# Moving a transformer layer's SBUF tiles so that every TensorE operand starts at a multiple of 256 bytes

## The chip, the core and the metric

The kernel runs on one core of one Trainium2 chip. The metric is device time in microseconds (us) of one execution; three runs of the kernel before gave 862.43, 862.78 and 863.02 us, and their median, 862.78 us, is the time before. A nanosecond (ns) is a thousandth of a us. The five engines are called PE (TensorE), DVE (VectorE), ACT (ScalarE), POOL (GpSimd) and SP (the engine that issues most DMAs). SBUF is the on-chip memory: 128 partitions, and in each a tile takes a run of bytes that begins at the same byte in all of them. That first byte is what this change is about.

## The reference, cut to what matters

```python
u = rms_norm(x, mix_norm_g)                       # x: 512 tokens x 1024 features, float32
q, k, v, cf_val, cf_gate, sc_x, sc_b, sc_c, gates = split(u @ w_in)
y_a = stick_breaking_attention(norm(q), norm(k), v) @ w_attn_out     # 8 heads of 64
hb  = silu(layer_norm(causal_conv_31(cf_val * sigmoid(cf_gate)) + dw_b))
y_b = hb @ w_conf_out
y_c = (sc_b * causal_conv_3(sc_c * sc_x)) @ w_sc_out
g   = sigmoid(gates + gate_b)
x   = x + (g[0] * y_a + g[1] * y_b + g[2] * y_c) @ w_o
gt, up = split(rms_norm(x, ffn_norm_g) @ w_ffn_in)                   # inner width 2816
x   = x + (silu(gt) * up) @ w_ffn_out
```

## The kernel before, in words

Every product is made of float32r operands: a float32 operand is split into a high and a low part (`split_to`, L75), and `mm3` (L87) multiplies high by high, high by low and low by high into one PSUM bank. In the profile the operands stand in the order moving, stationary: in `mm<-u,wh` the tile `u` streams through the array, 512 columns of it, while 128 columns of `wh` sit in it as weights. Each matmul comes with its own weight load (PEld in the profile).

Two helpers make nearly all matmuls. `unit` (L140) multiplies one block of 128 weight columns: the weights `wh` and `wl` are stationary, the activations move, in 24 matmuls where the contraction has 8 blocks of 128 and 12 where it has 4. `rows_product` (L629) and `values` (L364) do it the other way: activations are stationary and the weights move. The tiles on the activation side are

- `u` (16 tiles): the normed input, later the feed-forward's input. 96 units of 24 matmuls move it, and `values` holds it stationary in 96 matmuls: 2400 in all.
- `m` and `b` (18 and 8 tiles): everything else, that is queries and keys, the branches' inputs `oT`, `hb` and `hc`, the merged sum and the feed-forward's inner activations. 288 matmuls (three branches, 8 units of 12) move them, and `rows_product` holds them stationary in 720 (192 for `w_o`, 528 for `w_ffn_out`): 1008 in all.
- attention's own `l0`, `l1`, `l2`, `a` and `v`, and the constants `identr`, `big_ident`, `neg_tri`, `neg_ones`, `head_mean`; these take part in short matmuls of 128, 256 and 384 columns and in some 70 of 512.

PE's order is the order of the calls (`manual_schedule`, L163): input projections and the first norms, attention mixed with other units (`tick`, L99), the three branches, the output projection `w_o`, then twice a half of the feed-forward's input units and its `w_ffn_out`. The other engines are ordered by a scheduler with priorities. Weights come by DMA into `raw` (three buffers), ACT casts them to `wh`, DVE subtracts to `wl`.

Tiles are placed in the order in which their pools are opened, and within a pool in the order in which their tags first occur; each takes a whole number of 32 bytes. The kernel's first free byte is 16,512. Pool `cst` (L48) comes first and holds constants and parameter columns of odd sizes (4, 232, 496, 32, 16 bytes); pool `sb` (L49) follows with everything else. In `sb`, the tags `c` and `cf` have tiles of 2056 bytes (512 + 2 floats) and 2168 bytes (512 + 30 floats); all others are multiples of 512 bytes. So `cst` sets where `sb` begins, and each group of `c` or `cf` tiles shifts what follows it.

Of the kernel before, what the change touches and what calls it, by code (L numbers as in the profile page):

```python
# [8 lines left out]
F32 = mybir.dt.float32  # L9
F32R = mybir.dt.float32r  # L10
# [4 lines left out]
P = 128  # L15
S = 512
D = 1024
KT = D // P
# [3 lines left out]
EPS = 1e-6  # L22
# [13 lines left out]
def hybrid_layer(ctx, tc, x, mix_norm_g, w_in, q_norm_g, k_norm_g, w_attn_out, conf_dw_w,  # L36
                 conf_dw_b, conf_ln_g, conf_ln_b, w_conf_out, sc_conv_w, w_sc_out, gate_b,
                 w_o, ffn_norm_g, w_ffn_in, w_ffn_out, out):
    """Every product runs on the tensor engine as float32r operands: a float32 operand is the
    exact sum of a high and a low part of 12 significant bits each, and three passes  # L40
    (high*high, high*low, low*high) carry the product at float32's accuracy."""
    nc = tc.nc
    x, w_in, w_o = x[0], w_in[0], w_o[0]
    w_attn_out, w_conf_out, w_sc_out = w_attn_out[0], w_conf_out[0], w_sc_out[0]
    w_ffn_in, w_ffn_out, out = w_ffn_in[0], w_ffn_out[0], out[0]

    pool = lambda name, **kw: ctx.enter_context(tc.tile_pool(name=name, **kw))
    cst = pool("cst", bufs=1)  # L48
    sb = pool("sb", bufs=1)  # L49
    ps = pool("ps", bufs=1, space=PSUM)  # L50
    BUFS = {"raw": 3, "wh": 3, "wl": 3, "u": 16, "m": 18, "b": 8, "v": 2, "cf": 5, "c": 4, "t": 6,
            "s": 2, "a": 4, "l0": 2, "l1": 1, "l2": 1, "mm": 4, "z": 3, "o": 1}
# [1 line left out]

    def alloc(tag, shape=(P, S), dt=F32):
        count[0] += 1
        where = ps if tag in ("mm", "z", "o") else sb
        return where.tile(list(shape), dt, tag=tag, name=f"{tag}_{count[0]}", bufs=BUFS[tag])

    def psum(tag="mm"):  # L60
        return alloc(tag)

    def tmp(dt=F32, shape=(P, S)):
        return alloc("t", shape, dt)
# [4 lines left out]
    def exp_log():  # L69
        table(nc.scalar.preload_act_table_set("natural_log_exp_and_others"))  # L70

    def act(o, i, f, **kw):
        table(nc.scalar.activation(o, i, f, **kw))  # L73
# [10 lines left out]
    def mm(o, lhsT, rhs, start, stop):  # L84
        nc.tensor.matmul(o, lhsT, rhs, start=start, stop=stop, skip_group_check=True)  # L85

    def mm3(o, a, b, start, stop):  # L87
        mm(o, a[0], b[0], start, False)
        mm(o, a[0], b[1], False, False)
        mm(o, a[1], b[0], False, stop)  # L90

    # ---- the tensor engine's order is the order of the calls below: units of products come
    # from a queue in steps of one contraction block, with other products in between ----
    queue, later = [], []

    def defer(steps, fn):
# [23 lines left out]
        return  # L120
        yield

# [1 line left out]
    def raw(src, kt, width):  # L124
        with tc.high_priority():
            t = alloc("raw", (P, kt, width))
            nc.sync.dma_start(t, src.rearrange("(k p) n -> p k n", p=P))
        return t
# [3 lines left out]
    def wsplit(src):  # L132
        nsplit[0] += 1
        kt, n = src.shape[1], src.shape[2]
        with tc.high_priority():
            hi, lo = alloc("wh", (P, kt, n), F32R), alloc("wl", (P, kt, n), F32R)
            split_to(hi, lo, src, sub=nc.gpsimd.tensor_sub if nsplit[0] in POOLW else None)
        return hi, lo

    def unit(src, j, a, done):  # L140
        src, a = src(), a()
        w = wsplit(src[:, :, j * P:(j + 1) * P])
        kt = src.shape[1]
        o = psum()
        for k in range(kt):
            mm3(o, (w[0][:, k, :], w[1][:, k, :]), a[k], k == 0, k == kt - 1)
            if k == kt - 1:
                done(o)
            yield
# [12 lines left out]

    ctx.enter_context(tc.manual_schedule(engines={mybir.EngineType.PE}))  # L163

# [1 line left out]
    def load_x(tag):  # L166
        t = []
        for i in range(NT):
            t.append([alloc(tag) for _ in range(2)])
            for n in range(2):  # L170
                nc.sync.dma_start(t[i][n], x[i * P:(i + 1) * P, n * S:(n + 1) * S])  # L171
        return t
# [6 lines left out]

    rows_w = alloc("s", (P, P))  # L180
    rows = alloc("s", (P, P))
    rows_g = cst.tile([KT, P], F32, name="rows_g")
    nc.scalar.dma_start(rows_g, mix_norm_g[0].rearrange("(k p) -> k p", p=P))
    at = {}
    r = 0
# [16 lines left out]

    ident_f = alloc("c", (P, P))
    make_identity(nc, ident_f)
    identr = cst.tile([P, P], F32R, name="identr")
    nc.gpsimd.tensor_copy(identr, ident_f)
    ident = identr.bitcast(F32)
    big_ident = cst.tile([P, P], F32R, name="big_ident")
    nc.gpsimd.tensor_scalar_mul(big_ident, ident_f, BIG)
    eps = cst.tile([P, 1], F32, name="eps")  # L210
    nc.gpsimd.memset(eps, EPS)
# [10 lines left out]
        return cols[:, at[name] + i:at[name] + i + 1]  # L222

    def const(name, fill):
        t = cst.tile([P, P], F32R, name=name)
        f = tmp(shape=(P, P))
        fill(f)
        nc.gpsimd.tensor_copy(t, f)
        return t
# [13 lines left out]
            nc.gpsimd.memset(f[h * 64:(h + 1) * 64, h * 64:(h + 1) * 64], 1.0 / 64)  # L243

    def rsqrt(y, m, w):
        """y = (m + EPS) ** -0.5, one Newton step after the table's value; w: two tiles like y."""
        t, s = w
        act(t, m, AF.Ln, bias=eps)
        act(y, t, AF.Exp, scale=-0.5)
        nc.scalar.activation(s, y, AF.Square)  # L250
        nc.vector.scalar_tensor_tensor(t, m, eps, s, ALU.add, ALU.mult)
        nc.vector.tensor_scalar(t, t, -0.5, 1.5, ALU.mult, ALU.add)
        nc.vector.tensor_mul(y, y, t)

# [1 line left out]
    exp_log()  # L256
    transpose_rows(cols_g, rows_g, KT)
    uT = [(alloc("u", dt=F32R), alloc("u", dt=F32R)) for _ in range(KT)]
# [22 lines left out]
    neg_ones = const("neg_ones", filled(-1.0))  # L281
    head_mean = const("head_mean", heads)

# [1 line left out]
    cf = []  # L285
    marks = []

# [12 lines left out]
    gates = [unit(cfg[i // 2], i % 2, U, cf_gate) for i in range(CT)]  # L300
# [7 lines left out]
    transpose_rows(cols_w, rows_w, nw)  # L308
    drain()

# [1 line left out]
    own, other = [(0, 64), (64, 128)], [(64, 128), (0, 64)]  # L312
    pairs = [[[], []] for _ in range(NH // 2)]

# [43 lines left out]
                pairs[p][e].append(t1)  # L358
        return head_norm(col("k_g"), done)

# [1 line left out]
    vT = []  # L362

    def values():  # L364
# [15 lines left out]
                                     o[i].rearrange("p (h d) -> p h d", h=NH))  # L380
                        yield

    # ---- stick-breaking attention of one head, scores as [key, query]; a group of key tiles
    # shares one bank, each with the queries from its own first one on ----
    GROUPS = ((3, 2), (1,), (0,))

    def attend(h, oT):
# [61 lines left out]

        return scores, weights, mix  # L450

# [1 line left out]
    hc = []  # L453

    def conv(y, pad, width, w, b):
# [34 lines left out]
                yield unit(t, j, U, f(j))  # L490

    exp_log()
# [1 line left out]
    merged = {}  # L494
    mT = []

# [43 lines left out]
    steps = []  # L540
    NG = len(GROUPS)
    for i in range(NH * NG + 2):
        if i < NH * NG:
            h, g = divmod(i, NG)
            if g == 0:
                head = attend(h, oT[h // 2])
# [11 lines left out]
            with tc.high_priority(offset=PRIO):  # L558
                hd[2](g)

# [1 line left out]
    acc = []  # L562
    for i in range(CT):
        with tc.issue_after(marks[CONV_AT[i]].ins):
# [1 line left out]
                            lambda n: cols_w[:, n * CT + i:n * CT + i + 1], col("dw_b", i)))  # L566

    def mean(t, n):
        """The products of -1 and -t / n, summed over the partitions, in every partition."""
        h, l = tmp(F32R), tmp(F32R)  # L570
        nc.scalar.activation(h, t, AF.Copy, scale=-1.0 / n)
        nc.vector.scalar_tensor_tensor(l, t, -1.0 / n, h.bitcast(F32), ALU.mult, ALU.subtract)
        m = psum("z")

        def go():
            mm(m, neg_ones, h, True, False)
            mm(m, neg_ones, l, False, True)
        return m, go
# [3 lines left out]
    def conf_mean_start():  # L582
        t = tmp()
        nc.vector.tensor_add(t, acc[0], acc[1])
        for i in range(2, CT):
            nc.vector.tensor_add(t, t, acc[i])
        m, go = mean(t, C_CONF)

        def after():
            go()  # L590
            conf_var(m)
        defer(8, after)
# [32 lines left out]
    queue += branch(1, w_conf_out, lambda: hb, last=True)  # L625
    drain()

# [1 line left out]
    def rows_product(w, cs, a, banks, done, lag=0):  # L629
        """a: pairs [contraction block, token]; w: [contraction, column], columns cs."""  # L630
        n = len(a)
        o = [psum(tag) for tag in banks]
        for k0 in range(0, n, 4):
            kn = min(4, n - k0)
            wt = raw(w[k0 * P:(k0 + kn) * P, cs], kn, S)
            ws = [wsplit(wt[:, i:min(i + 2, kn), :]) for i in range(0, kn, 2)]
            order = [(k, i) for k in range(kn) for i in range(NT)]
            if k0 + kn == n:
                order = [(k, i) for i in range(NT) for k in range(kn)]
            for k, i in order:  # L640
                u = [part[:, i * P:(i + 1) * P] for part in a[k0 + k]]
                part = ws[k // 2]
                mm3(o[i], u, (part[0][:, k % 2, :], part[1][:, k % 2, :]), k0 + k == 0,
                    k0 + k == n - 1)
                if k0 + k == n - 1:
                    done(i, o[i])
                yield

    BANKS = (("mm",) * 4, ("z", "z", "z", "o"))

    # ---- output projection and residual; transposed for the feed-forward, whose norm scales
    # its products: the gains go in here, the squares are summed on the way ----
    x1 = []
    for n in range(2):
        t = alloc("v", (P, NT, S))
# [40 lines left out]
            rsqrt(rstd[0], m, (alloc("cf"), alloc("cf")))  # L696
        defer(8, after)

# [1 line left out]
    half = DFF // P // 2  # L700
    later_h = []

# [25 lines left out]
    for c in range(2):  # L728
# [9 lines left out]
        for n in range(2):  # L738
            cs = slice(n * S, (n + 1) * S)
# [42 lines left out]
```

## Time and profile before

| what | value |
|---|---|
| median of three runs | 862.78 us (862.43 to 863.02) |
| the profiled execution, first to last instruction (its span) | 860.7 us |
| the difference to the median, which lies around the span | 2.1 us |
| PE busy | 844.1 us (98%), 3817 matmuls |
| DVE, ACT, POOL busy | 514.9, 366.0, 19.6 us |
| granted TensorE clock | 1.000 |
| DMA | 81.45 MB, 95 GB/s in the mean |

The profiled execution has no time of its own beside its span. Busy times are of the profiled execution; a matmul counts from its start to its modelled end, and two or three are under way at once, so the time that a matmul costs is read from start to start (its step) and not from its duration. A stretch of the trace ("510.00:610.00") is in us from the first instruction. Groups of instructions are named by line of the kernel, engine and operation, with the tile written, an arrow and the tiles read.

### The profile page before, as it was taken

What the parts mean: (1) busy time and instruction counts of PE and PEld (TensorE: products, weight loads), DVE (VectorE), ACT (ScalarE), POOL (GpSimd) and SP (SyncE); (2) the same over time, 40 slices, a digit from 0 to 9 for tenths busy, and PEclk for the clock granted to TensorE, in tenths of its full rate; (3) what the DMA queues carried; (4) which work ended last, traced back from release to release, by engine and by line L of the source; (5) the groups of instructions that cost most, each with busy time, mean ns of one, the idle gap of its engine ahead of it and who ended that gap; (6) DMA issues with size and microseconds to landing.
All of it is one profiled execution on the core that took longest, in us unless ns stands there. A gap on an engine that the chain in (4) does not pass through costs nothing.

```text
span 860.7 us, 9550 instructions
## 1 busy us (share of the span) xinstructions
PE 844.1 (98%) x3817; PEld 697.3 (81%) x3817; DVE 514.9 (60%) x721; ACT 366.0 (43%) x543; POOL 19.6 (2%) x35
## 2 busy tenths in 40 slices
PE   5999999999999999999999999999999999999998
PEld 4888888888888888888888878888888888888886
DVE  5598699895899998774443454444422444444231
ACT  7346699876664233563332352333211222332120
POOL 4000000000000000000000120000000000000000
PEclk9999999999999999999999999999999999999999
DMA  8233114121113233232253223324224333223211
GB/s 269 78 99 113 34 54 143 49 92 56 50 49 98 76 121 97 73 125 97 98 196 98 65 82 99 99 73 131 78 86 136 108 98 98 73 71 130 93 50 50
DMA packets 71976, 81.45 MB, mean 95 GB/s; under 512 B 1600, under 2 KB 57084, under 8 KB 71932
## 3 DMA queue, kind: packets, MB, share of 16 engines
q1 hardware_dynamic: 70764, 78.74, 28.3%
q10 hardware_dynamic: 1168, 2.10, 0.7%
q8 instruction: 30, 0.49, 0.2%
q14 instruction: 14, 0.11, 0.0%
HBM read 78.74 MB, written 2.10 MB: 94 GB/s over the span
## 4 chain that ended last, share of the span: by engine, by line
PE 93%; DVE 4%; ACT 1%; DMA 1%; issue 1%; POOL 0%; POOLq 0%; SPq 0%; DVEq 0%; ACTq 0%
PE mm L85 75%; PE z L85 13%; PE o L85 4%; DVE cf L461 2%; DVE wl L77 1%; DMA m<-in_x_dram 1%; PE mm L272 0%; POOL cf L674 0%; PE mm L664 0%; POOLq L777 0%; ACT wh L76 0%; PE z L272 0%; ACT u L276 0%; ACT u L668 0%; SPq L171 0%
## 5 line engine op out<-in xcount | busy, mean ns | idle before, releaser
L85 PE MATMUL mm<-u,wh 128*128 128x512 f32 x1536 | 475.4, 390 | 1.3 <-DVE u L277 1.0
L85 PEld LDWEIGHTS mm<-u,wh 128*128 128x128 f32 x1536 | 287.0, 188 | 61.3 <-DVE u L277 1.6
L76 ACT CAST wh<-raw 128x1024 fp32r<-128x1024 f32 (+1 forms) x156 | 151.5, 973 | 383.9 <-PE mm L85 264.7
L85 PE MATMUL mm<-u,wl 128*128 128x512 f32 x768 | 299.4, 390 | 0.0
L77 DVE TENSOR_TENSOR wl<-raw,wh 128x1024 fp32r<-128x1024 f32 (+1 forms) x154 | 173.3, 1127 | 127.5 <-ACT wh L76 127.2
L85 PEld LDWEIGHTS mm<-u,wl 128*128 128x128 f32 x768 | 144.2, 188 | 30.1
L461 DVE SCALAR_TENSOR_TENSOR cf<-cf,cols_w,cf 128x512 f32<-128x512 f32 x120 | 89.8, 749 | 3.0 <-ACT cf L459 0.3
L85 PE MATMUL mm<-wh,m 128*128 128x512 f32 x176 | 56.6, 395 | 0.0
L717 DVE TENSOR_TENSOR t<-mm,cf 128x512 f32<-128x512 f32 x22 | 15.2, 691 | 68.6 <-PE mm L85 68.6
L85 PE MATMUL z<-wh,m 128*128 128x512 f32 x132 | 45.9, 397 | 0.0
L715 DVE TENSOR_TENSOR t<-mm,cf 128x512 f32<-128x512 f32 x22 | 15.2, 692 | 45.9 <-PE mm L85 45.9
L85 PE MATMUL mm<-m,wh 128*128 128x512 f32 x128 | 40.1, 394 | 0.0
L85 PEld LDWEIGHTS mm<-wh,m 128*128 128x128 f32 x176 | 33.1, 188 | 7.8
L85 PE MATMUL mm<-wl,m 128*128 128x512 f32 x88 | 34.7, 395 | 0.0
L85 PEld LDWEIGHTS z<-wh,m 128*128 128x128 f32 x132 | 24.9, 188 | 5.7
L85 PEld LDWEIGHTS mm<-m,wh 128*128 128x128 f32 x128 | 24.0, 188 | 5.5
L73 ACT ACTIVATE s<-s 128x384 f32<-128x384 f32 (+1 forms) x48 | 26.9, 560 | 1.1
L85 PE MATMUL z<-wl,m 128*128 128x512 f32 x66 | 26.0, 395 | 0.0
L85 PE MATMUL mm<-m,wl 128*128 128x512 f32 x64 | 25.3, 395 | 0.0
L413 DVE SCALAR_TENSOR_TENSOR s<-z,s 128x384 f32<-128x384 f32 (+1 forms) x24 | 14.3, 598 | 12.7 <-ACT s L73 12.5
L85 PE MATMUL mm<-wh,b 128*128 128x512 f32 x64 | 21.6, 395 | 0.0
L73 ACT ACTIVATE t<-t 128x512 f32<-128x512 f32 x31 | 19.4, 626 | 1.6 <-DVE t L715 1.5
(193 smaller groups left out, 865.5 us busy)
## 6 DMA issues: line engine op xcount, KB each, us to landing
raw<-in_w_in_dram SPq DMA_DIRECT2D x24, 1024.0 KB
raw<-in_w_ffn_in_dram SPq DMA_DIRECT2D x20, 1024.0 KB
raw<-in_w_ffn_out_dram SPq DMA_DIRECT2D x8, 1024.0 KB
raw<-in_w_in_dram SPq DMA_DIRECT2D x8, 512.0 KB
raw<-in_w_o_dram SPq DMA_DIRECT2D x4, 1024.0 KB
raw<-in_w_ffn_out_dram SPq DMA_DIRECT2D x4, 768.0 KB
m<-in_x_dram SPq DMA_DIRECT2D x8, 256.0 KB
raw<-in_w_sc_out_dram SPq DMA_DIRECT2D x2, 1024.0 KB
```

The costliest lines, as they stand in the source:

```text
L73: table(nc.scalar.activation(o, i, f, **kw))
L76: (copy or nc.scalar.copy)(hi, src)
L77: (sub or nc.vector.tensor_sub)(lo, src, hi.bitcast(F32))
L85: nc.tensor.matmul(o, lhsT, rhs, start=start, stop=stop, skip_group_check=True)
L413: marks.append(nc.vector.scalar_tensor_tensor(t, z, 0.0, t, ALU.max, ALU.add))
L461: nc.vector.scalar_tensor_tensor(y, pad[:, n:n + S], w(n), y, ALU.mult, ALU.add)
L715: nc.vector.tensor_mul(g, pg[0], rstd[0])
L717: nc.vector.tensor_mul(u, pu, rstd[0])
```

## The change

Two pools are put ahead of `cst`, one behind `sb`, and tiles are given to other pools. Pool `ops` comes first, with a pad of 128 bytes that brings its next tile to byte 16,640, and takes the small constants that PE reads (`rows_g`, `identr`, `big_ident`, `neg_tri`, `neg_ones`, `head_mean`, 512 bytes each). Then comes `sb`, without the tags `c` and `cf`, which go to the new pool `odd` behind it; `cst` with the odd-sized columns is last. Comments were taken out as well, with their lines left empty, and five new lines shift the line numbers by five. On all engines the instructions, their order, shapes and semaphore waits are those of before; only addresses differ.

```diff
@@ hybrid_layer
     pool = lambda name, **kw: ctx.enter_context(tc.tile_pool(name=name, **kw))
+    ops = pool("ops", bufs=1)
+    ops.tile([P, 32], F32, name="pad")
+    sb = pool("sb", bufs=1)
+    odd = pool("odd", bufs=1)
     cst = pool("cst", bufs=1)
-    sb = pool("sb", bufs=1)
     ps = pool("ps", bufs=1, space=PSUM)
...
-        where = ps if tag in ("mm", "z", "o") else sb
+        where = ps if tag in ("mm", "z", "o") else odd if tag in ("c", "cf") else sb
...
-    rows_g = cst.tile([KT, P], F32, name="rows_g")
+    rows_g = ops.tile([KT, P], F32, name="rows_g")
...
-    identr = cst.tile([P, P], F32R, name="identr")
+    identr = ops.tile([P, P], F32R, name="identr")
...
-    big_ident = cst.tile([P, P], F32R, name="big_ident")
+    big_ident = ops.tile([P, P], F32R, name="big_ident")
...
     def const(name, fill):
-        t = cst.tile([P, P], F32R, name=name)
+        t = ops.tile([P, P], F32R, name=name)
```

What this makes of the first bytes, read off the two built programs (the remainder of the first byte on division by 256; every part of a tile that PE reads lies a multiple of 512 bytes into it):

| tiles | before | after |
|---|---|---|
| `identr`, `big_ident`, `rows_g` | 128 | 0 |
| `neg_tri`, `neg_ones`, `head_mean` | 64 | 0 |
| `m`, `s` | 96 | 0 |
| `u`, `t`, `raw`, `wh`, `wl` | 224 | 0 |
| `v`, `b`, `l0`, `l1`, `l2`, `a` | 96 | 0 |
| `c` (4 tiles), which PE doesn't read | 96, 128, 160, 192 | 0, 32, 64, 96 |
| `cf` (5 tiles), which PE doesn't read | 224, 96, 224, 96, 224 | 128, 0, 128, 0, 128 |

## The prediction

> **What bounds the kernel now.** I read the page first: which engine is busy, at what clock, and what the last chain of waits is made of.
>
> ```profile
> span 860.7 us, 9550 instructions
> PE 844.1 (98%) x3817; PEld 697.3 (81%) x3817; DVE 514.9 (60%) x721; ACT 366.0 (43%) x543; POOL 19.6 (2%) x35
> PE   5999999999999999999999999999999999999998
> PEclk9999999999999999999999999999999999999999
> PE 93%; DVE 4%; ACT 1%; DMA 1%; issue 1%; POOL 0%; POOLq 0%; SPq 0%; DVEq 0%; ACTq 0%
> ```
>
> PE is busy for 98% of the span at the full granted clock, and 93% of the chain that ended last is PE. Of its 40 slices only the first is half empty, so other engines matter little after that, and the change is worth what it does to the cost of one matmul. The question is whether that cost depends on where in SBUF the operands start. The second view, PE's groups of instructions with their shapes kept apart, lets me ask this of the kernel before, because two starts occur in it: `u`, `wh` and `wl` begin at remainder 224 of 256, `m` and `b` at 96.
>
> ```profile
> L85 PE MATMUL mm<-u,wh 128*128 128x512 f32 x1536 | 475.4, 390 | 1.3 <-DVE u L277 1.0 <-DVE u L669 0.3
> L85 PE MATMUL z<-wh,u 128*128 128x512 f32 x48 | 16.1, 389 | 0.0
> L85 PE MATMUL mm<-wh,m 128*128 128x512 f32 x176 | 56.6, 395 | 0.0
> L85 PE MATMUL z<-wh,m 128*128 128x512 f32 x132 | 45.9, 397 | 0.0
> L85 PE MATMUL mm<-m,wh 128*128 128x512 f32 x128 | 40.1, 394 | 0.0
> L85 PE MATMUL mm<-wh,b 128*128 128x512 f32 x64 | 21.6, 395 | 0.0
> L85 PE MATMUL mm<-b,wh 128*128 128x512 f32 x64 | 20.0, 394 | 0.0
> L85 PE MATMUL o<-a,v 128*128 128x512 f32 x16 | 5.0, 392 | 0.0
> ```
>
> The shape is the same in all rows (128 x 512), and but for the last, to which I come back, the mean duration falls into two classes: 389 to 390 ns where both operands are at 224, 394 to 397 ns where one is at 96. It doesn't matter which of the two moves (`wh,u` is as fast as `u,wh`; `m,wh` as slow as `wh,m`), nor whether the tile is `m`, below `u` in SBUF, or `b`, far above it. These durations overlap, so the cost is the step from start to start. For that I take stretches in which PE never waits, one for each class (columns: stretch, its length, then busy time and count of each engine).
>
> ```profile
> 510.00:610.00 100.00, 100.00 (x443) 82.81 (x442) 47.24 (x58) 31.11 (x39) 0.00 (x0) 1.00 0.29 92
> 616.00:673.00 57.00, 57.00 (x247) 46.20 (x246) 16.63 (x18) 10.11 (x11) 0.00 (x0) 1.00 0.27 88
> 680.00:790.00 110.00, 110.00 (x487) 91.09 (x486) 50.37 (x60) 32.70 (x41) 0.00 (x0) 1.00 0.32 103
> 797.00:853.00 56.00, 56.00 (x243) 45.41 (x242) 15.20 (x17) 9.11 (x10) 0.00 (x0) 1.00 0.17 57
> 360.00:440.00 80.00, 80.00 (x351) 65.57 (x350) 44.62 (x61) 36.37 (x51) 0.00 (x0) 1.00 0.35 119
> ```
>
> A count takes in matmuls that overhang an edge. One lasts 390 ns against a step of 227, so 1.7 are open at any moment and the count is 1.7 too high. Feed-forward input (`u` with `wh`): 100 us / 441.3 = 226.6 ns, and 110 / 485.3 = 226.7. `w_ffn_out` (`m` and `b` with `wh`): 57 / 245.3 = 232.4 and 56 / 241.3 = 232.1. The branches (of 36 matmuls 24 are `u` with `wh`, 12 are `m` or `b` with `wh`): 80 / 349.3 = 229.0; if the 24 take 226.7, the 12 take 226.7 + 3 x 2.3 = 233.6. The timeline shows how even the fast class is:
>
> ```profile
> 599.94 0.62 PE L85 MATMUL mm<-u,wh 128*128 128x512 f32 x2
> 600.39 0.39 PE L85 MATMUL mm<-u,wl 128*128 128x512 f32 x1
> 600.62 0.62 PE L85 MATMUL mm<-u,wh 128*128 128x512 f32 x2
> 601.08 0.39 PE L85 MATMUL mm<-u,wl 128*128 128x512 f32 x1
> 601.30 0.62 PE L85 MATMUL mm<-u,wh 128*128 128x512 f32 x2
> ```
>
> Six matmuls from 599.94 to 601.30 are 1.36 us, 226.7 each, in the middle of DVE, ACT and DMA work: those leave no mark. So PE's cost depends on its own two operands.
>
> **The change part by part.** What the rows show is that a pair whose two operands begin at the same remainder of 256 is cheaper by 5.5 to 7 ns than a pair that begins 128 bytes apart. The change makes all pairs alike.
>
> 1. `w_o` and `w_ffn_out`, 720 matmuls: 232.3 (mean of 232.4 and 232.1) goes to 226.7, 5.6 ns x 720 = 4.0 us.
> 2. Products of the branches, 288: 233.6 to 226.7, 6.9 ns x 288 = 2.0 us.
> 3. Some 70 matmuls of 512 columns in attention and with the constants, at about 5 ns: 0.3 us.
> 4. Short matmuls of attention. Here some pairs were equal before (`a` and `v`, both 96) and some were 32 bytes apart (`l` at 96, the constants at 64):
>
> ```profile
> 162.16 0.62 PE L85 MATMUL z<-l,neg_ones 128*128 128x128 f32 x4
> 162.61 0.51 PE L85 MATMUL z<-l,neg_tri 128*128 128x384 f32 x2
> 165.71 0.62 PE L85 MATMUL o<-a,v 128*128 128x128 f32 x4
> 166.18 0.23 PE L85 MATMUL z<-m,m 128*128 128x128 f32 x1
> ```
>
> The same four shapes take 0.45 us apart (162.16 to 162.61) and 0.47 equal (165.71 to 166.18): equality costs up to 0.02 us for four. Some 260 short matmuls make 65 fours, so the term lies between nothing and 1.3 us of loss; I take 0.3, near the lower end, because the two fours differ by little more than the rows' rounding.
>
> 5. `u` with `wh`, 2400 matmuls, and `a` with `v`: they were equal and stay equal; only the remainder itself goes from 224 (or 96) to 0. No row has a 512-column pair at 0, so its price is bounded by the rivals below; I take nothing, because `a` with `v`, equal at 96, lasts 392 ns in the second view and `u` with `wh`, equal at 224, 390: both stand at the fast end, whatever the remainder is that they share.
> 6. DVE and ACT read and write at new places as well. The 31-tap convolution reads the same tile at 30 successive offsets of 4 bytes, and stays even:
>
> ```profile
> L461 DVE SCALAR_TENSOR_TENSOR cf<-cf,cols_w,cf 128x512 f32<-128x512 f32 x120 | 89.8, 749 | 3.0 <-ACT cf L459 0.3
> ```
>
> So nothing there, and it would lie beside PE's work in any case. `c` and `cf` lose nothing by standing elsewhere.
> 7. DMAs land at new starts. Only the first wait of the kernel is at stake:
>
> ```profile
> 2.65 5.14 DMA m<-in_x_dram
> ```
>
> That is 5.14 us of the chain, with nothing in the trace that ties it to the start byte: I take 0. The Trainium skill (DMA: Bandwidth & Descriptors, How a descriptor splits into AXI transactions) has transfers that begin off a 256-byte boundary split into one transaction more; a row of 2048 bytes would need 8 in place of 9, by which an estimated ninth, 0.6 us, of that stretch could go. No row here shows it.
>
> Sum: -4.0 - 2.0 - 0.3 + 0.3 = -6.0 us. The span goes from 860.7 to 854.7; the median stands 2.1 us above the span (862.78 against 860.7), so 856.8 us. PE stays the bound: it works through without a wait in every stretch above, and a gain of 6 us in 850 changes no cover. The bounds of this case by itself are 855 (the short matmuls lose nothing, 0.3, and the `u` matmuls that stand among attention's, by the program's order some 480 in the stretch of 100 to 250 us, are freed of what a neighbour of another class costs them, at most the 2.3 ns between the branches' mean and the fast class: 1.1) and 858.5 (the short matmuls at their worst, 1.0 more, and 5.5 ns for all 1008, 0.5 less gain).
>
> One rule speaks against terms 1 to 3. The rows first: 226.7 against 232.3, by nothing but which tiles are paired. The Trainium skill (TensorE: Matmul & The Clock Gate, Part 2: What happens when you issue a matmul) says that moving operand and weight load have read ports of their own, and that loading the next weights takes no read bandwidth from the running matmul. By that alone a pair's remainders could not matter together, and the sum would be nothing. The trace does not agree, by 5.6 ns a matmul; but the rule keeps the second rival below alive.
>
> **The rivals.** *The start itself counts, not only the pair.* Then the 2400 gain too. For it: 226.7 ns is not the array's best. The transpositions of 128 columns move `identr`, which already begins at a multiple of 128:
>
> ```profile
> L664 PE MATMUL mm<-identr,v 128*128 128x128 f32 x28 | 3.9, 272 | 0.0
> 493.54 0.60 PE L664 MATMUL z<-identr,v 128*128 128x128 f32 x4
> ```
>
> Four take 0.60 us, the last one 0.27 of it, so the step is 0.33 / 3 = 109 ns. If an f32 operand passes twice through the array (an assumption; as float32r it passes once), that is 256 columns in 109 ns, and 512 in 218. Then 2400 x 8.7 + 720 x 14.3 + 288 x 15.6 = 35.7 us, 827.1. Twice 109 holds two change-overs where one matmul has one; with one of 3 ns less, 215 ns, it is 2400 x 11.7 + 720 x 17.3 + 288 x 18.6 = 45.9, 816.9. Against it: f32 may not be read as float32r is, the 109 ns may be the weight load's and not the stream's, and between 96 and 224 the shared remainder made next to no difference. The Trainium skill (TensorE: Matmul & The Clock Gate, Wait — 56ns, not 53.3ns?) gives N / 2.4 + 2.5 ns for back-to-back matmuls, 215.7 ns at 512 columns; the trace, at 226.7, does not reach it, and by the rule the time would be an estimated 819. DVE would not get in the way:
>
> ```profile
> 100.00:250.00 150.00, 150.00 (x766) 128.60 (x765) 128.97 (x209) 116.58 (x201) 0.53 (x3) 1.00 0.22 71
> ```
>
> With PE 5% shorter this densest stage would be 143 us against DVE's 129.
>
> *The classes have another cause.* `m` and `b` could be slow because of what wrote them, or because of the order of matmuls around them. Against it: `u` with `wh` and `b` with `wh` come out of the same helper, one after the other, in the branches. Then all stays: 862.8.
>
> *The start at 0 is a worse one for equal pairs.* Two streams that begin at remainder 0 together could meet in a way that those at 224 avoid. The place is the 2400 `u` matmuls. If they settle at 232.3, as unequal pairs do, and the 1008 stay, the loss is 5.6 x 2400 = 13.4 us, 876.2. It decides against the forecast's own gain of 6.0 from 6.0 / 2400 = 2.5 ns on, at a step of 229.2. For it: the start has never been at 0, so nothing excludes it. Against it: neither of the two equal remainders in the trace is slow.
>
> That the layout is not what the change says can be left out, since the first bytes are read off the built program.
>
> **How the numbers follow.** Equal pairs gain and the rest stays (856.8): 0.45, since every stretch without a wait bears it out and it needs nothing that isn't in a row. The start counts as well (817 to 827): 0.36; it rests on one kind of instruction, but the trace leaves room for it. Another cause (862.8): 0.10. Worse at 0 (876): 0.09. The range of 816 to 860 takes in the first two, 0.81 of the chance, with their bounds; the likeliest case by itself is 855 to 858.5. A change under 0.2% (1.7 us, about what a measurement of this kernel can tell from none) counts as the same: faster 0.45 + 0.36 = 0.81, same 0.10, slower 0.09.
>
> **What would show it right or wrong.** Right: the stretches of `w_ffn_out` at a step of 226.7 and groups `mm<-wh,m` and `mm<-m,wh` at 390 ns like `mm<-u,wh`, which itself is unchanged. The first rival: `mm<-u,wh` falls below 389 ns and the feed-forward's stretches shrink. The second: 395 and 390 stay as they are. The third: `mm<-u,wh` above 392. Wrong in any case if PE begins to wait inside a stage, or DVE's and ACT's durations move.

## The result, and the profile after

| | before | after |
|---|---|---|
| median | 862.75 us (862.43 to 863.02, 4 runs) | 855.94 us (855.70 to 856.85, 4 runs) |
| span of the profiled execution | 860.7 us | 853.7 us |

The ratio of after to before is 0.9925, with a 95% interval of 0.9911 to 0.9939: the kernel is faster by 6.8 us. The prediction's likeliest case was 856.8, within 855 to 858.5.

The page of after, its span, the busy times and the chain that ended last by engine:

```profile
span 853.7 us, 9550 instructions
PE 837.0 (98%) x3817; PEld 696.3 (82%) x3817; DVE 514.6 (60%) x721; ACT 365.8 (43%) x543; POOL 19.8 (2%) x35
PE 93%; DVE 4%; ACT 1%; DMA 1%; issue 1%; POOL 0%; POOLq 0%; SPq 0%; DVEq 0%; ACTq 0%
```

PE has lost 7.1 us of busy time and the span 7.0; DVE, ACT and the chain's shares are what they were. So nothing new waits: the matmuls themselves became cheaper. Which ones, is told by the groups of PE with their shapes kept apart:

```profile
L90 PE MATMUL mm<-u,wh 128*128 128x512 f32 x1536 | 475.1, 390 | 1.3 <-DVE u L282 1.0 <-DVE u L674 0.3
L90 PE MATMUL mm<-wh,m 128*128 128x512 f32 x176 | 55.6, 389 | 0.0
L90 PE MATMUL z<-wh,m 128*128 128x512 f32 x132 | 45.2, 392 | 0.0
L90 PE MATMUL mm<-m,wh 128*128 128x512 f32 x128 | 39.4, 389 | 0.0
L90 PE MATMUL mm<-wh,b 128*128 128x512 f32 x64 | 21.2, 389 | 0.0
L90 PE MATMUL mm<-b,wh 128*128 128x512 f32 x64 | 19.7, 389 | 0.0
```

The two classes of before are gone. `u` with `wh` stands where it stood; each group with `m` or `b` fell by 5 or 6 ns. The durations overlap, so the price is again read from stretches in which PE doesn't wait, the same five stages and then the densest one:

```profile
505.00:605.00 100.00, 100.00 (x443) 82.81 (x442) 47.45 (x58) 30.61 (x39) 0.00 (x0) 1.00 0.29 92
610.00:667.00 57.00, 57.00 (x253) 47.20 (x252) 18.09 (x20) 11.25 (x12) 0.00 (x0) 1.00 0.30 100
673.00:783.00 110.00, 110.00 (x487) 91.10 (x486) 50.72 (x61) 32.60 (x40) 0.00 (x0) 1.00 0.32 103
790.00:846.00 56.00, 56.00 (x249) 46.37 (x248) 16.43 (x19) 10.08 (x11) 0.00 (x0) 1.00 0.18 65
355.00:435.00 80.00, 80.00 (x355) 66.23 (x354) 45.36 (x63) 38.92 (x54) 0.00 (x0) 1.00 0.34 118
100.00:250.00 150.00, 150.00 (x766) 128.80 (x765) 129.15 (x209) 116.67 (x201) 0.53 (x3) 1.00 0.22 71
```

With 1.7 taken off each count: the feed-forward's input 100 / 441.3 = 226.6 and 110 / 485.3 = 226.7 ns, as before; `w_ffn_out` 57 / 251.3 = 226.8 and 56 / 247.3 = 226.4 (232.4 and 232.1 before); the branches 80 / 353.3 = 226.4 (229.0). One count more or less is 0.5 to 0.9 ns, so these five stretches now have one step. The densest one, among attention's products, holds 766 matmuls in 150 us as it did before: little was gained there.

The two executions run the same 3817 matmuls in the same order, and each of those below is recorded in both, so that the start of the same matmul shows where the 7 us were gained:

| the matmul that starts at (before, us) | what ended there | after minus before, us | gained in this part |
|---|---|---|---|
| 16.96 | the first norm, before PE works through | -0.33 | 0.33 |
| 33.03 | the first input projections | -0.43 | 0.10 |
| 268.81 | attention and the units in it | -0.89 | 0.46 |
| 442.94 | the branches | -2.75 | 1.86 |
| 493.90 | `w_o` | -3.87 | 1.12 |
| 614.00 | first half of the feed-forward's input | -3.87 | 0.00 |
| 675.58 | first `w_ffn_out` | -5.39 | 1.52 |
| 795.07 | second half of the input | -5.42 | 0.03 |
| 856.42 (the last matmul) | second `w_ffn_out` | -6.94 | 1.52 |

### The profile page after: what moved, and what is told of

It is laid out like the page before. It is cut to its first block, busy times and chain, and to the rows that moved or that the text cites. A ratio compares the mean times of both kernels' runs of the same rounds, so it can differ in the third digit from the quotient of the medians.

```text
span 853.7 us, 9550 instructions
## 1 busy us (share of the span) xinstructions
PE 837.0 (98%) x3817; PEld 696.3 (82%) x3817; DVE 514.6 (60%) x721; ACT 365.8 (43%) x543; POOL 19.8 (2%) x35
## 4 chain that ended last, share of the span: by engine, by line
PE 93%; DVE 4%; ACT 1%; DMA 1%; issue 1%; POOL 0%; POOLq 0%; SPq 0%; DVEq 0%; ACTq 0%
PE mm L90 75%; PE z L90 13%; PE o L90 4%; DVE cf L466 2%; DVE wl L82 1%; DMA m<-in_x_dram 1%; PE mm L277 0%; POOL cf L679 0%; PE mm L669 0%; POOLq L782 0%; ACT wh L81 0%; ACT u L281 0%; ACT u L673 0%; SPq L176 0%; PE z L277 0%
## 5 line engine op out<-in xcount | busy, mean ns | idle before, releaser
L78 ACT ACTIVATE t<-t 128x512 f32<-128x512 f32 x31 | 19.5, 628 | 1.6 <-DVE t L720 1.5
```

## The experiments

Three theories were open. *Pair*: a matmul costs more when the first bytes of its two operands differ in the remainder by 256, whatever that remainder is. *Start*: each operand is cheap at some starts (0 above all) and dear at others. *Place*: `m` and `b` were dear because of where they lie or what lies beside them, and the new order of the pools cured that. All kernels are after with a few lines changed, and each ratio is to before on the same chip. In most of them a pool `far` behind `sb` takes some tags, and the pad of `ops` is left out, so that what PE reads from elsewhere stands at remainder 128.

**All operands at remainder 160.** The pad is 32 bytes in place of 128, so that everything moves together.

```diff
-    ops.tile([P, 32], F32, name="pad")
+    ops.tile([P, 8], F32, name="pad")
```

> All operands of TensorE stay equal, but at remainder 160 of 256 in place of 0 (a pad of 32 bytes in place of 128). Pair theory (only the difference of the two operands' first bytes counts): as the changed kernel, 856 us within 1, step of the feed-forward's matmuls 226.7 ns. Start theory (multiples of 256 are what helps): 862 us or more, since no operand begins at a multiple of 256 any longer. Region theory (it was the new place in SBUF at large): as the changed kernel, since the places differ by 96 bytes only.

Measured: 855.95 us (855.49 to 856.81), ratio to before 0.9918 [0.9901, 0.9934], the time of after. Its groups of PE (line, tiles, shape, count, then busy time and mean ns of one)

```profile
L90 PE MATMUL mm<-u,wh 128*128 128x512 f32 x1536 | 475.0, 390 | 1.3 <-DVE u L282 1.0 <-DVE u L674 0.3
L90 PE MATMUL mm<-wh,m 128*128 128x512 f32 x176 | 55.6, 389 | 0.0
```

and a stretch of the second half of the feed-forward's input and one of `w_ffn_out`:

```profile
680.00:780.00 100.00, 100.00 (x443) 82.81 (x442) 45.36 (x54) 29.35 (x36) 0.00 (x0) 1.00 0.31 100
800.00:850.00 50.00, 50.00 (x222) 41.40 (x221) 13.31 (x15) 7.46 (x8) 0.00 (x0) 1.00 0.19 69
```

100 / 441.3 = 226.6 and 50 / 220.3 = 227.0 ns. So a multiple of 256 is not what brings the gain; the operands share a remainder here as in after. *Start* falls.

**`u` alone 128 bytes off.** `u` is at remainder 0, all else at 128.

```diff
-    ops.tile([P, 32], F32, name="pad")
     sb = pool("sb", bufs=1)
+    far = pool("far", bufs=1)
+    far.tile([P, 32], F32, name="pad")
...
+        where = far if tag in ("u",) else where
```

> Only the tiles u are moved, behind all other operands, to remainder 0 while the rest is at 128. Pair theory: the 2400 matmuls of u with wh or wl go from 226.7 to between 232.3 and 233.6 ns, which is 13.4 to 16.6 us: 869 to 873 us. Start theory: u is now at a multiple of 256 and the weights are not; half of the pair as before, so about 862. Region theory: u lies far up in SBUF, above the weights; nothing tells how much, and the 1008 others stay.

Measured: 869.51 us (869.00 to 869.64), ratio 1.0075 [1.006, 1.009], 13.6 us above after. Its groups

```profile
L92 PE MATMUL mm<-u,wh 128*128 128x512 f32 x1536 | 482.8, 395 | 1.3 <-DVE u L284 1.0 <-DVE u L676 0.3
L92 PE MATMUL mm<-wh,m 128*128 128x512 f32 x176 | 55.7, 389 | 0.0
```

and the same two stretches:

```profile
680.00:780.00 100.00, 100.00 (x430) 80.47 (x429) 45.22 (x53) 29.09 (x36) 0.00 (x0) 1.00 0.28 88
800.00:850.00 50.00, 50.00 (x222) 41.33 (x221) 14.88 (x16) 9.97 (x11) 0.00 (x0) 1.00 0.23 79
```

The classes have changed sides: the input's step is 100 / 428.3 = 233.5 ns, that of `w_ffn_out` 227.0. The 13.6 us over 2400 matmuls are 5.7 ns each. `u` stands at remainder 0 here, the value that the change aims at, and is dear.

**`m` and `b` alone 128 bytes off**: the relation of before in the new order of pools. The same lines, with `where = far if tag in ("m", "b") else where`.

> The old relation alone: m and b 128 bytes away from the rest (m, b at 0, the rest at 128), all else equal. Pair theory: the gain is undone, 1008 x 6 ns = 6 us, 862 us, with w_ffn_out at a step of 232.3 ns and the feed-forward's input at 226.7. Start theory: m and b are at multiples of 256, u and the weights are not, so the feed-forward's input gets slower. Region theory: as the changed kernel plus or minus what the new place costs.

Measured: 862.37 us (861.68 to 863.45), ratio 0.9994 [0.9984, 1.0003]: before's time is back. Its groups

```profile
L92 PE MATMUL mm<-u,wh 128*128 128x512 f32 x1536 | 475.2, 390 | 1.1 <-DVE u L284 0.8 <-DVE u L676 0.3
L92 PE MATMUL mm<-wh,m 128*128 128x512 f32 x176 | 56.7, 395 | 0.0
```

and the stretch of `w_ffn_out`:

```profile
800.00:850.00 50.00, 50.00 (x217) 40.52 (x216) 12.46 (x13) 8.49 (x9) 0.00 (x0) 1.00 0.17 58
```

`w_ffn_out` is at 50 / 215.3 = 232.2 ns. One of the kernel's differences, undone alone, takes the whole gain away.

**`m` and `b` in the same place, 256 bytes off.** The pool `far` begins with the 232-byte tile `cols`, which fills 256 bytes, in place of the pad.

```diff
-    ops.tile([P, 32], F32, name="pad")
...
+    far = pool("far", bufs=1)
+    cols = far.tile([P, 58], F32, name="cols")
...
+        where = far if tag in ("m", "b") else where
...
-    cols = cst.tile([P, nr], F32, name="cols")
```

> The same places as in the run before but m and b 256 bytes away from the rest and not 128 (the cols tile of 256 bytes stands ahead of them): equal remainders of 256, unequal of 512. Pair theory with a period of 256 bytes: as the changed kernel, 856 us within 1. With a longer period (512, 2048): slower, towards 862. Region theory: the same as the run before, since m and b lie within 128 bytes of where they lay there.

Measured: 856.36 us (856.23 to 856.91), ratio 0.9925 [0.9911, 0.994]. Its groups:

```profile
L92 PE MATMUL mm<-wh,m 128*128 128x512 f32 x176 | 55.7, 389 | 0.0
L92 PE MATMUL mm<-m,wh 128*128 128x512 f32 x128 | 39.4, 389 | 0.0
```

128 bytes further, 6.0 us less. *Place* falls, and a difference of 256 counts as none where one of 128 is dear: that fits a period of 256 and no longer one.

**How the price depends on the distance.** `wh` and `wl` alone are moved, so that all 3408 long products with a split weight are unequal: by 32, 64 and 128 bytes (pads of 8, 16 and 32 floats at the head of `far`, tags `("wh", "wl")`), and by 32 bytes the other way, with `far` opened ahead of `sb` and the pad at the head of `sb`:

```diff
-    ops.tile([P, 32], F32, name="pad")
+    far = pool("far", bufs=1)
     sb = pool("sb", bufs=1)
+    sb.tile([P, 8], F32, name="pad")
...
+        where = far if tag in ("wh", "wl") else where
```

> All weight tiles (wh, wl) 32 bytes on from everything else: 3408 pairs, the 2400 of u and the 1008 of m and b, have a difference of 32. If any difference costs what 128 did (5.6 to 6.9 ns): 3408 x 6 = 20 us above the changed kernel, 876 us. If the cost grows with the distance round a circle of 256 bytes: a quarter of it, 861. If only bit 7 of the address counts: 856.

> The same with 64 bytes. Any difference alike: 876 us. Growing with the distance: half, 866. Only bit 7: 856.

> The same with 128 bytes: every theory of the pair says 5.6 to 6.9 ns for each of 3408, 19 to 24 us, 875 to 880 us. It fixes the size for all matmuls at once.

> Weights 32 bytes below everything else (a difference of 224, or minus 32). If the circle is symmetric: as the run with 32. If it matters which operand is ahead, the two differ, and one of them could be faster than equal pairs: at 224 ns a matmul, the quickest step seen for 512 columns in the trace of before, it would be 3408 x 2.7 = 9 us below the changed kernel, 847.

| weights moved by | median, us | ratio to before, 95% | above after, over 3408 |
|---|---|---|---|
| 32 bytes | 876.66 | 1.0159 [1.0142, 1.0176] | 20.7 us, 6.1 ns |
| 64 bytes | 874.15 | 1.0130 [1.0115, 1.0145] | 18.2 us, 5.3 ns |
| 128 bytes | 875.44 | 1.0145 [1.0130, 1.0160] | 19.5 us, 5.7 ns |
| -32 bytes | 876.50 | 1.0158 [1.0143, 1.0173] | 20.6 us, 6.0 ns |

The four kernels ran on another chip, where before took 862.34 us, 0.4 less than in the result; that is 0.1 ns in the last column. The price hardly grows with the distance: 32 bytes cost as much as 128, and the hope that some distance would be better than none is gone. The smaller sum at 64 comes from one kind of pair. The groups at 32 bytes

```profile
L92 PE MATMUL mm<-u,wh 128*128 128x512 f32 x1536 | 484.2, 396 | 1.3 <-DVE u L284 1.0 <-DVE u L676 0.3
L92 PE MATMUL mm<-wh,m 128*128 128x512 f32 x176 | 56.8, 396 | 0.0
```

and a stretch of `w_ffn_out`:

```profile
815.00:865.00 50.00, 50.00 (x216) 40.24 (x215) 12.89 (x14) 8.40 (x9) 0.00 (x0) 1.00 0.17 58
```

The groups at 64 bytes, with one more of them

```profile
L92 PE MATMUL mm<-u,wh 128*128 128x512 f32 x1536 | 484.1, 396 | 1.4 <-DVE u L284 1.1 <-DVE u L676 0.3
L92 PE MATMUL mm<-wh,m 128*128 128x512 f32 x176 | 56.1, 392 | 0.0
L92 PE MATMUL mm<-m,wh 128*128 128x512 f32 x128 | 40.3, 396 | 0.0
```

and the same stretch:

```profile
815.00:865.00 50.00, 50.00 (x221) 41.06 (x220) 12.73 (x15) 7.43 (x8) 0.00 (x0) 1.00 0.18 64
```

At 32 bytes both kinds are dear (50 / 214.3 = 233.3 ns for `w_ffn_out`). At 64 the pair is dear when the weights are held (`m,wh`, 396) but nearly free when they move (`wh,m`, 392; 50 / 219.3 = 228.0 ns, one count in this short stretch being 1 ns; the mean from start to start over `w_o` and `w_ffn_out` is 229.0 ns, against 233.3 at 32 bytes and 226.9 after). So at 64 the two kinds differ: the moving operand is ahead of the stationary one in the cheap kind and behind it in the dear one. At 128, where ahead and behind are the same, both are dear. Whether the sign of the distance decides, or the starts themselves (192 for the weights, 128 for the rest), would take a run with 64 bytes the other way; why 64 is an exception isn't settled.

**Operands of two bytes.** What is left of a pair's cost when nothing differs, 226.7 ns, is still above the 215.7 ns of the Trainium skill's rule that the prediction weighed (TensorE: Matmul & The Clock Gate, Wait — 56ns, not 53.3ns?). Two kernels give the feed-forward's input bfloat16 parts in place of float32r ones, one in after's layout, one with the weights 128 bytes off besides:

```diff
-        hi, lo = alloc("u", dt=F32R), alloc("u", dt=F32R)
+        hi, lo = alloc("u", dt=BF16), alloc("u", dt=BF16)
...
-                yield unit(wg, j, lambda: u2, pg.append)
-                yield unit(wu, j, lambda: u2, up)
+                yield unit(wg, j, lambda: u2, pg.append, BF16)
+                yield unit(wu, j, lambda: u2, up, BF16)
```

> The layout of after; in the feed-forward's input alone (1,056 of the 3,817 matmuls) both operands are rounded to bfloat16 high and low parts instead of float32r ones, so that the output is computed less precisely there; everything else as after. Two theories of the 226.7 ns that are left when the remainders are equal. If the step is set by how fast 4-byte operands can be read, 2-byte ones are fetched faster: the step there falls to about 216 ns (the Trainium skill, page TensorE: Matmul & The Clock Gate, section Wait - 56ns, not 53.3ns?, gives 215.7 for 512 columns), 1,056 x 11 ns = 11.6 us, about 844 us in all if nothing else becomes late. If the step belongs to the column stream whatever the type: 226.7 ns stays, and 856 us.

> As the bfloat16 kernel beside it, with wh and wl moved 128 bytes, so that every pair of a split weight and its moving operand has unequal remainders. If the extra time of an unequal pair belongs to 4-byte reads, the bfloat16 matmuls of the feed-forward's input show none: the same step there as in the kernel beside it, while the other 2,350 long matmuls with a split weight pay some 6 to 7 ns each: about 14 to 16 us slower than the kernel beside it. If it belongs to every pair: 6 to 7 ns in the feed-forward's input too, and 20 us slower, as the 19.5 us between the float32r kernels.

Measured: 844.82 us (844.37 to 845.41), ratio 0.9794 [0.9779, 0.9809], and 856.82 us (856.62 to 857.99), ratio 0.9936 [0.9920, 0.9953]. The groups of the first, with their type,

```profile
L91 PE MATMUL mm<-u,wh 128*128 128x512 bf16 x690 | 206.7, 379 | 1.3 <-DVE u L675 0.4
L91 PE MATMUL mm<-u,wl 128*128 128x512 bf16 x344 | 130.4, 379 | 0.4
```

and the first and last row of a stretch of its timeline (start, duration, and two matmuls to a row where it ends in x2):

```profile
690.21 0.59 PE L91 MATMUL mm<-u,wh 128*128 128x512 bf16 x2
...
769.85 0.38 PE L91 MATMUL mm<-u,wh 128*128 128x512 bf16 x1
```

The groups of the second:

```profile
L93 PE MATMUL mm<-u,wh 128*128 128x512 bf16 x690 | 206.7, 379 | 1.3 <-DVE u L677 0.4
L93 PE MATMUL mm<-u,wl 128*128 128x512 bf16 x344 | 130.4, 379 | 0.4
L93 PE MATMUL mm<-wh,m 128*128 128x512 f32 x176 | 57.0, 397 | 0.0
```

Some bfloat16 matmuls are missing from both traces (1034 of 1056 are there), so the step comes from the long stretch: 363 start in it, seven gaps between neighbours are two steps long, and 79.64 us / 369 = 215.8 ns. The 215.7 of the Trainium skill holds here. 1056 x (226.7 - 215.8) = 11.5 us; the runs differ by 11.1. And the 128 bytes that cost a float32r pair 5.7 ns cost these nothing: 206.7 us and 379 ns in both kernels, while `wh,m` of the second is at 397. The 12.0 us between the two fall on the other 2352 products, 5.1 ns each, less than the 14 to 16 expected; the first kernel's long matmuls began later by 0.9 us (17.45 against 16.56 us), with which it is 5.5 ns each. So the step of 226.7 ns is that of float32r operands, and so is the extra of a pair 128 bytes apart; 32 and 64 bytes were not tried with bfloat16. Which of the two operands brings it isn't separated, because both change their type, and the weight load becomes shorter with it, 98 ns against 188 in the first of the two kernels:

```profile
L91 PEld LDWEIGHTS mm<-u,wh 128*128 128x128 f32 x832 | 154.9, 188 | 31.9 <-DVE u L283 1.6
L91 PEld LDWEIGHTS <-wh 128*128 128x128 bf16 x704 | 68.6, 98 | 83.0 <-issue 0.7 <-ACT wh L82 0.3
```

## Why the prediction was right

Its first case came about. **Terms 1 and 2**, the whole of the forecast gain, hold in mechanism: `w_o` and `w_ffn_out` were to give 4.0 us and their stages gave 1.12 + 1.52 + 1.52 = 4.16; the branches were to give 2.0 and their stage gave 1.86.

The two traces also tell this matmul by matmul, if each is given the time from its start to the next start and the two times are subtracted. The 720 of term 1 gained 4.10 us, 5.7 ns each. The 288 of term 2 gained 1.70 us, 5.9 ns each and not 6.9: 36 of them run among attention's (0.19 us), 252 in the branches' stage (1.51 us), and the `u` products between those gained 0.33 us more. So the step of 233.6 ns was read too high, because the `u` products in the branches were taken to be at 226.7 already; the stage's gain was put down to 12 matmuls in 36 where part of it was their neighbours'. That the cause is the pair was an argument from two classes in one trace; the kernels with `m` and `b` 128 and 256 bytes off now show it, since between them nothing differs in the order of PE's work.

**Terms 3 and 4** were to cancel, a gain of 0.3 against a loss of 0.3; both are near nothing. Term 3 counted 70 matmuls, but 32 of them (`m` with `m`, `a` with `v`) were equal pairs before; all 70 together gained 0.11 us. In term 4 the same holds for 96 of the short ones. The loss from equal short pairs was read off 0.45 against 0.47 us. After the change, where both fours are equal pairs, the timeline has them at

```profile
161.59 0.62 PE L90 MATMUL z<-l,neg_ones 128*128 128x128 f32 x4
162.05 0.52 PE L90 MATMUL z<-l,neg_tri 128*128 128x384 f32 x2
...
165.15 0.62 PE L90 MATMUL o<-a,v 128*128 128x128 f32 x4
165.61 0.22 PE L90 MATMUL z<-m,m 128*128 128x128 f32 x1
```

0.46 us each: the difference was the rows' rounding. All 272 short matmuls of attention changed by 0.01 us together, so term 4 is nothing. The 0.46 us that attention's stretch gained are 0.19 from the 36 branch products in it, 0.20 from the products of `u`, which the prediction had bounded at 1.1, and 0.10 from the long matmuls of term 3 in it.

**Terms 5 and 6** are nothing, as forecast, but for what the `u` products gained beside unequal pairs: the two halves of the feed-forward's input gained 0.00 and 0.03 us, and the convolution stands where it stood:

```profile
L466 DVE SCALAR_TENSOR_TENSOR cf<-cf,cols_w,cf 128x512 f32<-128x512 f32 x120 | 89.9, 749 | 3.0 <-ACT cf L464 0.3
```

**Term 7**, the first DMAs, was put at nothing, and the first long matmul came 0.33 us earlier:

```profile
16.63 0.72 PE L90 MATMUL mm<-u,wh 128*128 128x512 f32 x2 [0.86 <-DVE u L282]
```

That cannot be put down to the layout. The same matmul starts at 16.96 us before, and between 16.56 and 17.71 in the ten experiments; the latest (17.71) has `m`, into which the first rows land, 128 bytes off a multiple of 256, but with it at 0 it starts at 16.98 and at 17.45 as well. The stretch of the first load itself did not become shorter; after the change it is

```profile
2.66 5.25 DMA m<-in_x_dram
```

against 5.14 us before. So the 0.6 us that the prediction estimated from the Trainium skill (DMA: Bandwidth & Descriptors, How a descriptor splits into AXI transactions) are not seen; in the ten experiments the stretch takes 4.82 to 5.80 us, and both ends of that range have `m` at remainder 128.

The sum came out at 6.94 us at the last matmul (6.8 in the medians) against 6.0; the 0.9 more are attention and the start (0.33 + 0.10 + 0.46), which the prediction held at nothing in net, and of these the 0.33 cannot be put down to the layout. By its own terms its bounds would be 855.4 and 858.3 where it says 855 and 858.5; 855.94 lies within both. The median stands 855.94 - 853.7 = 2.2 us above the span; 2.1 was assumed.

**The rivals.** *The start itself counts too* had 0.36. `mm<-u,wh` at 390 ns and an unchanged input stage refute it, and all operands at 160 again. Its evidence was the transpositions' 109 ns, whose row is unchanged although their operands went from remainders 128 and 96 to 0 and 0:

```profile
L669 PE MATMUL mm<-identr,v 128*128 128x128 f32 x28 | 3.9, 272 | 0.0
```

So they say nothing of the start. The step that they hinted at, 215 to 218 ns for 512 columns, exists, but the bfloat16 run shows that it is reached by another type of operand; none of the starts tried (0, 128, 160, 224) reaches it with float32r. *Another cause* falls with the kernels in which `m` and `b` move by 128 bytes more. *Worse at 0* falls with the 0.00 us of the input stage, though the size that it put on a dear `u`, 13.4 us, is what 128 bytes cost it (13.6).

**The rule weighed.** The Trainium skill (TensorE: Matmul & The Clock Gate, Part 2) says that the weight load takes no read bandwidth from the running matmul, and the prediction drew from it that a pair's remainders could not matter together. For float32r they do: a shift of `u` alone is 5.7 ns a matmul. For bfloat16 a shift of the weights by 128 bytes costs nothing. Whether the rule itself fails for float32r, the extra time being a meeting of the two reads, was not shown; no run here takes the weight load away from a long float32r product and keeps the rest.

## What to carry to other kernels

Before a layout is changed, split PE's groups by operands and shape and compare the steps of the classes in stretches without a wait: two classes of one shape are a price list that the kernel already carries. For float32r products that run back to back, give the moving and the stationary operand the same remainder of 256 in SBUF; among 0, 128, 160 and 224 it made no difference which. So one odd-sized tile ahead of some operands and not of others is what to look for. Where the precision allows bfloat16 parts, the step was 215.8 ns with the operands equal or 128 bytes apart; other distances were not tried.

## What the runs showed of the hardware that was not expected

- The price of an unequal pair is nearly a step and not a slope: 6.1 ns a matmul at 32 bytes, 5.7 at 128, 6.0 at -32, all of a 226.7 ns step.
- At 64 bytes, with the weights the higher ones, a pair is nearly free when the weights move (229.0 ns a step, 392 ns long) and as dear as at 32 bytes when they are held (396 ns long).
- A float32r matmul of 512 columns steps at 226.4 to 227.0 ns with equal remainders, in the mean of a stretch, whichever remainder was tried; a bfloat16 one at 215.8, and the latter doesn't pay for 128 bytes.
